# A transformer layer's seam of branch and output products: gates' products ahead of low parts, the last merged tile by halves, VectorE and ScalarE in written order into the first pair

## The chip, the cores and the metric

The kernel runs on one core of a Trainium2 chip, in one launch. The time is device microseconds, the median of several runs. The engines of the core are named as the profile names them: PE (TensorE, matrix products; PEld is its weight load), DVE (VectorE), ACT (ScalarE), POOL (GpSimd) and SP (SyncE, which issues most transfers). Each engine works through its own queue in order and waits by semaphores for the others. Products accumulate in PSUM, tiles live in SBUF, weights and inputs in HBM.

## The reference, cut to what matters

One layer of a diffusion transformer in float32, 1024 tokens by 1024 channels: two attention branches (windowed A, global B), merged by sigmoid gates, an output projection, a layer norm, and a convolutional feed-forward net with a second layer norm. The change lies where the branches are merged and projected:

```python
def _merge_branches(o_a, o_b, gate_logits, w_branch_a, w_branch_b, w_out):
    g_a, g_b = jnp.split(jax.nn.sigmoid(gate_logits), 2, axis=-1)
    return (g_a * (o_a @ w_branch_a) + g_b * (o_b @ w_branch_b)) @ w_out
...
        y = _latent_token_mixer(h, kv_ctx, w_in[l], ...)
        x = _layer_norm(DEEPNORM_ALPHA * x + gate1 * y, ln1_g[l], ln1_b[l])
```

## The kernel before, in words

**Layout.** Channels lie on the 128 partitions, so the 1024 channels are eight tiles, numbered f = 0 to 7, each 128 x 1024 (tokens along the row). The two token halves of 512 are hsl(0) and hsl(1); slice(0, T) is the whole row.

**Float32 by three products.** A float32 operand is split into a high part (a cast to a shorter format, `fp32r`) and a low part (the operand less its high part). `split` (L368 the cast, L373 the low part) does this for weights. `mm3` multiplies high by high (L376), high weight by low operand (L377) and low weight by high operand (L378).

**Branch products and merge.** `bT[0, f]` holds gate A times branch A's product already. `bT[1, f]` is loaded with gate B's sigmoid (the tiles sgd). For f = 0 to 3 only the second token half of branch B's product is left when the seam begins: `group` makes it in PSUM, `gmul` (L1117) multiplies it into `bT[1, f]` on DVE. For f = 4 to 7 `both` makes both halves (tile b, 24 matmuls of 512 columns), and L1418 multiplies it by the gate. Then `merge` adds the two branches on DVE (L1369) and casts the sum to its high part mh on ACT (L1371), and `msplit` makes the low part ml on DVE (L1376). "Gate f" below means this product of tile f.

**The output product.** y = merged times w_out: `y_pair(f, s)` makes two of the eight output tiles for the token range s, in one PSUM tile, with mh and ml of all eight merged tiles as operands. The first pair goes for both of its outputs through merged tiles 0 to 5 first and then through 6 and 7. The weight of output f is loaded as rwo, cast to hwo on ACT (L368), its low part lwo made on DVE (L373), all by `wout_start(f)`, which also loads two tiles of x, z (L1364), and scales them on POOL (L1365): L1532 adds y to them later, and the first layer norm follows.

**Slots.** `ht` hands out the oldest free one of some 35 SBUF slots, `hput` returns one. A load into a slot waits for the last reader of what lay there.

**What sets the order.** Inside a `manual_schedule` block the engines named keep the order in which the code is written; elsewhere a scheduler orders each queue. Before, one block, branch, holds all five engines from the split of w_b's weights up to the last msplit; PE alone is held again from just ahead of the output products.

**nmod and grd.** L1956 makes a small tile nmod (used by the second layer norm at the end of the kernel), and L1983 stores half of it transposed, in pieces of four bytes, to the DRAM tile grd.

Of the kernel before, what the change touches and what calls it, by code (L numbers as in the profile page):

```python
# [7 lines left out]
F32 = mybir.dt.float32  # L8
R32 = mybir.dt.float32r
AF = mybir.ActivationFunctionType  # L10
ALU = mybir.AluOpType
# [4 lines left out]
T = 1024  # L16
NC = 256
KT = 8
# [335 lines left out]
def layer_kernel(  # L354
# [6 lines left out]
    nc = tc.nc  # L361
# [59 lines left out]
    def ht(name, shape=(P, T), dt=F32):  # L421
        hslot[name] = pool, tag = hfree.pop(0)
        return pool.tile(list(shape), dt, tag=tag, name=name, bufs=1)

    def hput(*names):
        for n in names:
            hfree.append(hslot.pop(n))
# [51 lines left out]
    def hsl(hf):  # L479
        return slice(hf * HALF, (hf + 1) * HALF)  # L480
# [39 lines left out]
    for n in (0, 1):  # L520
        s = slice(n * HALF, (n + 1) * HALF)
# [11 lines left out]
    for k in range(KT):  # L533
# [5 lines left out]
        for t in range(NT):  # L539
            s = slice(t * P, (t + 1) * P)  # L540
# [436 lines left out]
    order = []  # L977
# [22 lines left out]
    for n, (gi, k, a) in enumerate(steps):  # L1000
# [21 lines left out]
        for t in tiles:  # L1022
            if t < NT:
                s = slice(t * P, (t + 1) * P)
                x = hT[k][0][:, s], hT[k][1][:, s]
            else:
                s = slice((t - NT) * P, (t - NT + 1) * P)
# [67 lines left out]
    bT, wab, bacc = {}, {}, {}  # L1095
# [252 lines left out]
    mrg = []  # L1348
    zt_ = {}

    def zv(f, s):
        hf = s.start // HALF
        return zt_[f % 4, hf][:, f // 4, s.start - hf * HALF:s.stop - hf * HALF]
# [3 lines left out]
    def wout_start(f, rtag="raw"):  # L1357
        wts[f] = weight(w_out[f], f"wo{f}", 8, tag=None if f < 4 else "wd" if f & 2 else "w", he=nc.scalar,
                        le=nc.vector, rtag=rtag)
        for hf in (0, 1):  # L1360
            if f < 4:
                zt_[f, hf] = ht(f"z{f}_{hf}", (P, 2, HALF))
            z = zv(f, hsl(hf))
            nc.sync.dma_start(z, xT[f][:, hsl(hf)])  # L1364
            nc.gpsimd.tensor_scalar(out=z, in0=z, scalar1=ALPHA, scalar2=0.0, op0=ALU.mult, op1=ALU.add)  # L1365

    def merge(f):
        m = bT[0, f]
        nc.vector.tensor_tensor(out=m, in0=m, in1=bT[1, f], op=ALU.add)  # L1369
        mh, ml = ht(f"mh{f}", dt=R32), ht(f"ml{f}", dt=R32)  # L1370
        nc.scalar.copy(mh, m)  # L1371
        mrg.append((mh, ml))

    def msplit(f):
        mh, ml = mrg[f]
        nc.vector.tensor_tensor(out=ml, in0=bT[0, f], in1=mh.bitcast(F32), op=ALU.subtract)  # L1376
        hput(f"bT0_{f}", f"bT1_{f}")

    wb = {2: [wq.tile([P, 8, P], R32, tag="w", name=f"{a}wb2", bufs=4) for a in "hl"]}
    branch = ExitStack()  # L1380
    branch.enter_context(tc.manual_schedule(engines={mybir.EngineType.PE, mybir.EngineType.DVE, mybir.EngineType.SP,
                                                     mybir.EngineType.Activation, mybir.EngineType.Pool}))
    split(rwb[2], *wb[2], nc.scalar, nc.gpsimd)
    hput("rwb2")

    def both(f):
        ps = big(f"b1_{f}")
        w = wb[f // 2]
        for hf in (0, 1):
            for j in range(4):  # L1390
                k = (f % 2) * 4 + j
                a = O[1, hf, 0, j // 2][:, j % 2], O[1, hf, 1, j // 2][:, j % 2]
                mm3(ps[:, hsl(hf)], (w[0][:, k], w[1][:, k]), a, j == 0, j == 3)
        return ps
# [7 lines left out]
    for f in range(KT):  # L1402
        if f < 4:
            group(1, f, 1, sml(f"b1_{f}_1"))
            gmul(1, f, 1)
            if f:
                msplit(f - 1)
            if f == 1:
                wb[3] = weight(w_b[3], "wb3", 8, he=nc.scalar, le=nc.gpsimd, rtag=None)
            if f == 3:  # L1410
                later(6)
                later(7)
        else:
            ps = both(f)
            msplit(f - 1)
            if f in (5, 7):
                wout_start(f // 2 - 2, None)
            nc.vector.tensor_tensor(out=bT[1, f], in0=ps, in1=bT[1, f], op=ALU.mult)  # L1418
        merge(f)
    msplit(KT - 1)  # L1420
    branch.close()
    opool.release()

    post = tc.alloc_tile_pool(name="post", bufs=1, side="left", reuse_waits="tile")
# [207 lines left out]
    def y_pair(f, s, first=False):  # L1632
        w = s.stop - s.start
        ps = big(f"y{f}_{s.start}_{w}")
        for ks in (range(6), range(6, KT)) if first and s.start == 0 else (range(KT),):
            for a in (0, 1):
                mm_ticked(ps[:, a * HALF:a * HALF + w], wts[f + a], mrg, s, ks)
        for a in (0, 1):
            wout_z(f + a, s, ps[:, a * HALF:a * HALF + w], first and a == 0)

    def ln1(si):
        return ln_steps(zs, zq, LN1_S[si], f"a{si}", emit1, LN1_F[si], *LN1_D[si], order=(0, 4, 1, 5, 2, 6, 3, 7))

    order = ctx.enter_context(ExitStack())
    order.enter_context(tc.manual_schedule(engines={mybir.EngineType.PE}))
    for f in range(0, KT, 2):
        if f + 2 < KT:
            for a in (2, 3):
                wout_start(f + a)
        y_pair(f, hsl(0), f == 0)  # L1650
    pend += ln1(0)
    for f in (0, 2):
        y_pair(f, hsl(1), f == 0)
# [131 lines left out]
    for k in range(4):  # L1785
        steps = build(k)
        n = 2 if k < 2 else 0
# [244 lines left out]
    s = LN2_S[-1]  # L2032
# [181 lines left out]
```

## Time and profile before

| what | value |
|---|---|
| median of 3 runs | 1527.97 us (1526.24 to 1531.01) |
| the profiled execution | 1527.93 us, span 1526.1 us |
| mean granted TensorE clock | 0.998 |
| PE busy | 1510.1 us, 99% |
| DVE busy | 1146.5 us, 75% |
| ACT, POOL busy | 799.2 us, 779.4 us |
| last products of branch B (tile b) | from 735.7 us to 768.3 us after the start |
| first output pair (tile y) | from 768.3 us to 782.8 us |

All times on the timeline are microseconds from the span's start. In a row of the timeline stand start, duration, engine, line, operation, output and inputs (without buffer numbers), shape, and in brackets the idle time before it and what ended it. In the list of waits stand who waited for whom, the total, how often, and the longest.

### The profile page before, as it was taken

The page shows a single profiled execution, that of the slowest core. Times are in us where ns is not written, and L with a number is a line of the kernel's source. Part 1 is how long each engine was busy: PE and PEld are TensorE (multiplying, and loading weights), DVE is VectorE, ACT ScalarE, POOL GpSimd, SP SyncE. Part 2 cuts the span into 40 slices and gives each one's busy share as a digit, 9 for nine tenths or more (in the row PEclk, how much of TensorE's full clock was granted, in tenths as well). Part 3 has the DMA queues.
Part 4 walks back from the last instruction along what each step waited for, and adds up shares of the span by engine and source line. Part 5 has one row for each costly group of instructions (what it writes and reads, how often), then busy time and mean ns, then how long its engine had stood idle before and what let it go on. Part 6 is the DMA issues. An engine that isn't in the chain of part 4 may idle for free.

```text
span 1526.1 us, 21981 instructions
## 1 busy us (share of the span) xinstructions
PE 1510.1 (99%) x7652; PEld 1269.0 (83%) x7652; DVE 1146.5 (75%) x1727; ACT 799.2 (52%) x1403; POOL 779.4 (51%) x743
## 2 busy tenths in 40 slices
PE   9999999999999999999999999999999999999997
PEld 7888888889988888888878998888888888888786
DVE  7588847629777777787656888888888887657797
ACT  5422223449987777788233574444444444435533
POOL 0365303428896566585513556666676664021063
PEclk9999999999999999999999999999999999999999
DMA  9667663312447654723460323333344446996723
GB/s 378 242 230 255 213 233 118 100 38 68 116 112 179 169 126 103 179 59 113 145 154 30 108 83 110 111 111 110 111 110 111 109 111 191 370 270 205 249 83 111
DMA packets 112161, 229.73 MB, mean 151 GB/s; under 512 B 13521, under 2 KB 27345, under 8 KB 111954
## 3 DMA queue, kind: packets, MB, share of 16 engines
q1 hardware_dynamic: 97040, 199.72, 39.8%
q0 software_dynamic: 10400, 20.19, 8.6%
q10 hardware_dynamic: 4610, 8.42, 1.5%
q8 instruction: 60, 0.98, 0.3%
q14 instruction: 51, 0.42, 0.1%
HBM read 177.09 MB, written 65.87 MB: 159 GB/s over the span
## 4 chain that ended last, share of the span: by engine, by line
PE 90%; DVE 4%; DMA 2%; POOL 1%; issue 1%; ACT 1%; SPq 0%; DVEq 0%; POOLq 0%; ACTq 0%
PE av L851 7%; PE pt L842 6%; PE g L378 4%; PE g L377 4%; PE g L376 4%; PE p L377 3%; PE p L378 3%; PE p L376 3%; PE s L754 3%; PE s L755 3%; PE c L377 2%; PE d L377 2%; PE a L377 2%; PE c L376 2%; PE d L376 2%; PE a L376 2%
## 5 line engine op out<-in xcount | busy, mean ns | idle before, releaser
L1226 DVE TENSOR_TENSOR lo<-pt,hi 128x512 fp32r<-128x512 f32 x188 | 126.8, 687 | 44.1 <-ACT hi L1220 33.8
L373 DVE TENSOR_TENSOR ld<-rd,hd 128x1024 fp32r<-128x1024 f32 x77 | 97.5, 1284 | 50.2 <-ACT hd L368 48.1
L1220 ACT CAST hi<-pt 128x512 fp32r<-128x512 f32 x188 | 108.3, 581 | 42.0 <-PE pt L842 23.1
L368 ACT CAST hd<-rd 128x1024 fp32r<-128x1024 f32 x77 | 79.5, 1050 | 86.1 <-PE p L378 59.1
L851 PE MATMUL av<-hi,VT 128*128 128x512 f32 x236 | 104.2, 443 | 0.2 <-POOL hi L1215 0.2
L377 PE MATMUL p<-ld,hd 128*128 128x512 f32 x264 | 102.8, 390 | 0.9 <-DVE ld L373 0.9
L376 PE MATMUL p<-hd 128*128 128x512 f32 x264 | 103.4, 392 | 0.0
L378 PE MATMUL p<-hd,ld 128*128 128x512 f32 x264 | 102.7, 389 | 0.0
L378 PE MATMUL g<-hh,wlg 128*128 128x512 f32 x256 | 99.7, 390 | 0.4 <-POOL wlg L373 0.4
L376 PE MATMUL g<-hh,whg 128*128 128x512 f32 x256 | 100.0, 390 | 0.0
L377 PE MATMUL g<-hl,whg 128*128 128x512 f32 x256 | 99.6, 389 | 0.0
L851 PE MATMUL av<-lo,VT 128*128 128x512 f32 x236 | 99.3, 422 | 0.1
L373 POOL TENSOR_TENSOR wlg<-wg,whg 128x512 fp32r<-128x512 f32 x32 | 45.1, 1413 | 103.4 <-ACT whg L368 98.7
L788 DVE TENSOR_SCALAR_CACHE_REDUCE p<-s,cvt,nmc 128x1024 f32<-128x1024 f32 x64 | 85.6, 1339 | 11.0 <-PE s L755 7.0
L842 PEld LDWEIGHTS pt<-ident,p 128*128 128x128 f32 x512 | 63.5, 140 | 17.6 <-ACT rb L824 0.4
L797 ACT ACTIVATE p<-p,nm 128x1024 f32<-128x1024 f32 x64 | 73.9, 1155 | 7.0 <-DVE p L788 6.5
L842 PE MATMUL pt<-ident,p 128*128 128x128 f32 x512 | 76.6, 272 | 0.1
L368 ACT CAST wS<-s 128x512 fp32r<-128x512 f32 x76 | 45.3, 620 | 53.3 <-POOL s L1546 52.5
L754 PE MATMUL s<-KL,q 128*128 128x512 f32 (+2 forms) x186 | 72.9, 392 | 0.0
L788 DVE TENSOR_SCALAR_CACHE_REDUCE pa<-s,negsink 128x640 f32<-128x640 f32 (+1 forms) x58 | 49.3, 853 | 29.2 <-PE s L755 28.7
L755 PE MATMUL s<-KL,q 128*128 128x512 f32 (+2 forms) x186 | 69.5, 374 | 0.0
L368 ACT CAST wA<-ru 128x512 fp32r<-128x512 f32 x57 | 35.5, 623 | 59.6 <-PE d L378 31.2
(436 smaller groups left out, 5034.4 us busy)
## 6 DMA issues: line engine op xcount, KB each, us to landing
wml<-in_wmodT_dram SPq DMA_DIRECT2D x48, 512.0 KB
ru<-in_w_up_dram SPq DMA_DIRECT2D x38, 512.0 KB
rd<-td SPq DMA_DIRECT2D x55, 256.0 KB
rd<-sd SPq DMA_DIRECT2D x44, 256.0 KB
rd<-in_w_dn_dram SPq DMA_DIRECT2D x33, 256.0 KB
wm<-in_wmodT_dram SPq DMA_DIRECT2D x16, 512.0 KB
wg<-in_w_g_dram SPq DMA_DIRECT2D x32, 256.0 KB
q<-q SPq DMA_DIRECT2D x64, 128.0 KB
```

What stands on the lines that cost most here:

```text
L368: cast[:] = [nc.scalar.copy(hi, src).ins]
L373: low[:] = [lo_eng.tensor_tensor(out=lo, in0=src, in1=hi.bitcast(F32), op=ALU.subtract).ins]
L376: nc.tensor.matmul(ps, a[0], b[0], start=start, stop=False, skip_group_check=resumed)
L377: nc.tensor.matmul(ps, a[0], b[1], start=False, stop=False, skip_group_check=resumed)
L378: return nc.tensor.matmul(ps, a[1], b[0], start=False, stop=stop, skip_group_check=resumed).ins
L754: nc.tensor.matmul(o, self.q1[:, hs], ks, start=True, stop=False)
L755: nc.tensor.matmul(o, self.q2[:, hs], ks, start=False, stop=stop)
L788: nc.vector.tensor_scalar(out=p if self.br else p[:, self.pad + 1:SINK + 1], in0=self.sv[h], scalar1=self.scale()[:, hs] if self.br else - ...
L842: nc.tensor.transpose(tr[:, h * P:(h + 1) * P], src, ident)
L851: nc.tensor.matmul(self.av, v, self.parts[n][low], start=first, stop=self.left == 0)
L1220: nc.scalar.copy(hi, units[u].parts[n])
L1226: e.tensor_tensor(out=lo, in0=src, in1=hi.bitcast(F32), op=ALU.subtract)
```

## The change

Four things are rewritten, and no product is added or removed.

- For f = 4 to 7 the product is multiplied by the gate ahead of the previous tile's low part, no longer behind it.
- The last tile (f = 7) goes through multiplication, merge, cast and low part in two halves of 512 tokens.
- The first two output weights are started in other places: w_out 0 behind merge 4, w_out 1 ahead of gate 6's product, each before in the middle of tiles 5 and 7.
- The written order now holds DVE and ACT into the first pair of y, SP and POOL as before up to the last msplit, and PE without a gap. So five small operations on modc and lnx, which the scheduler used to put far earlier, now stand behind the last ml.

```diff
-    def merge(f):
+    def merge(f, s):
         m = bT[0, f]
-        nc.vector.tensor_tensor(out=m, in0=m, in1=bT[1, f], op=ALU.add)
-        mh, ml = ht(f"mh{f}", dt=R32), ht(f"ml{f}", dt=R32)
-        nc.scalar.copy(mh, m)
-        mrg.append((mh, ml))
-
-    def msplit(f):
+        if s.start == 0:
+            mrg.append((ht(f"mh{f}", dt=R32), ht(f"ml{f}", dt=R32)))
+        nc.vector.tensor_tensor(out=m[:, s], in0=m[:, s], in1=bT[1, f][:, s], op=ALU.add)
+        nc.scalar.copy(mrg[f][0][:, s], m[:, s])
+
+    def msplit(f, s=slice(0, T)):
         mh, ml = mrg[f]
-        nc.vector.tensor_tensor(out=ml, in0=bT[0, f], in1=mh.bitcast(F32), op=ALU.subtract)
-        hput(f"bT0_{f}", f"bT1_{f}")
+        nc.vector.tensor_tensor(out=ml[:, s], in0=bT[0, f][:, s], in1=mh[:, s].bitcast(F32), op=ALU.subtract)
+        if s.stop == T:
+            hput(f"bT0_{f}", f"bT1_{f}")
 
-    branch = ExitStack()
-    branch.enter_context(tc.manual_schedule(engines={mybir.EngineType.PE, mybir.EngineType.DVE, mybir.EngineType.SP,
-                                                     mybir.EngineType.Activation, mybir.EngineType.Pool}))
+    order = ctx.enter_context(ExitStack())
+    order.enter_context(tc.manual_schedule(engines={mybir.EngineType.PE}))
+    branch, inner = ExitStack(), ExitStack()
+    branch.enter_context(tc.manual_schedule(engines={mybir.EngineType.DVE, mybir.EngineType.Activation}))
+    inner.enter_context(tc.manual_schedule(engines={mybir.EngineType.SP, mybir.EngineType.Pool}))
...
         else:
+            if f == 6:
+                wout_start(1, None)
             ps = both(f)
-            msplit(f - 1)
-            if f in (5, 7):
-                wout_start(f // 2 - 2, None)
-            nc.vector.tensor_tensor(out=bT[1, f], in0=ps, in1=bT[1, f], op=ALU.mult)
-        merge(f)
-    msplit(KT - 1)
-    branch.close()
+            for s in [hsl(0), hsl(1)] if f == KT - 1 else [slice(0, T)]:
+                nc.vector.tensor_tensor(out=bT[1, f][:, s], in0=ps[:, s], in1=bT[1, f][:, s], op=ALU.mult)
+                if s.start == 0:
+                    msplit(f - 1)
+                merge(f, s)
+            if f == 4:
+                wout_start(0, None)
+            continue
+        merge(f, slice(0, T))
+    for n in (0, 1):
+        msplit(KT - 1, hsl(n))
+    inner.close()
...
-    order = ctx.enter_context(ExitStack())
-    order.enter_context(tc.manual_schedule(engines={mybir.EngineType.PE}))
     for f in range(0, KT, 2):
         if f + 2 < KT:
             for a in (2, 3):
                 wout_start(f + a)
         y_pair(f, hsl(0), f == 0)
+        if f == 0:
+            branch.close()
```

PE's own order stays the same, row for row. The other queues move as follows; in the names, the last number is a buffer number.

DVE at the end of the branch, before: the last two gates (bT1_7 out of b1_7 is the multiplication, bT0_7 the merge), the low parts ml, and the low parts of output weights lwo.

```order
L1376 TENSOR_TENSOR ml6_8830<-bT0_6_5361,mh6_8829 128x1024
L373 TENSOR_TENSOR lwo1_8861<-rwo1_8858,hwo1_8860 128x1024
L1418 TENSOR_TENSOR bT1_7_8721<-b1_7_8832,bT1_7_8721 128x1024
L1956 TENSOR_SCALAR nmod_13047<-modc_60 128x8
L1369 TENSOR_TENSOR bT0_7_5724<-bT0_7_5724,bT1_7_8721 128x1024
L373 TENSOR_TENSOR lwo2_8893<-rwo2_8890,hwo2_8892 128x1024
L1376 TENSOR_TENSOR ml7_8873<-bT0_7_5724,mh7_8872 128x1024
L373 TENSOR_TENSOR lwo3_8905<-rwo3_8902,hwo3_8904 128x1024
```

DVE at the same place now, from the multiplication of gate 7's first half on (lwo1 stands four rows ahead of it).

```order
L1421 TENSOR_TENSOR bT1_7_8725<-b1_7_8848,bT1_7_8725 128x512
L1966 TENSOR_SCALAR nmod_13054<-modc_60 128x8
L1376 TENSOR_TENSOR ml6_8845<-bT0_6_5361,mh6_8844 128x1024
L1371 TENSOR_TENSOR bT0_7_5724<-bT0_7_5724,bT1_7_8725 128x512
L1421 TENSOR_TENSOR bT1_7_8725<-b1_7_8848,bT1_7_8725 128x512
L1371 TENSOR_TENSOR bT0_7_5724<-bT0_7_5724,bT1_7_8725 128x512
L1376 TENSOR_TENSOR ml7_8876<-bT0_7_5724,mh7_8875 128x512 x2
L1436 TENSOR_SCALAR modc_60<-modc_60 128x8
L1437 TENSOR_TENSOR lnx_68<-ln1c_66,modc_60 128x8
L1438 TENSOR_TENSOR lnx_68<-ln1c_66,modc_60 128x8
L1439 TENSOR_TENSOR lnx_68<-lnx_68,modc_60 128x8
L1440 TENSOR_SCALAR lnx_68<-ln1c_66 128x16
```

lwo2 follows behind these rows: ml7 now stands ahead of it, in halves, and the five small operations between.

ACT at the same place, before: casts of merged tiles (mh) and of output weights (hwo).

```order
L1371 CAST mh5_8798<-bT0_5_5058 128x1024
L1371 CAST mh6_8829<-bT0_6_5361 128x1024
L368 CAST hwo1_8860<-rwo1_8858 128x1024
L368 CAST hwo2_8892<-rwo2_8890 128x1024
L1371 CAST mh7_8872<-bT0_7_5724 128x1024
```

ACT now.

```order
L1372 CAST mh5_8801<-bT0_5_5058 128x1024
L368 CAST hwo1_8807<-rwo1_8805 128x1024
L1372 CAST mh6_8844<-bT0_6_5361 128x1024
L1372 CAST mh7_8875<-bT0_7_5724 128x512 x2
L368 CAST hwo2_8898<-rwo2_8896 128x1024
```

hwo1 moved ahead of mh6, and hwo2 behind mh7.

SP before, from the load of z for outputs 3 and 7 on (rwo are output weights, z tiles of x, grd the store of nmod).

```order
L1364 DMA z3_1_8911<-in_xT_dram 128x512 x2
L1333 DMA rwo2_8890<-in_w_out_dram 128x1024
L1333 DMA rwo3_8902<-in_w_out_dram 128x1024
L1364 DMA z3_0_8908<-in_xT_dram 128x512
L1333 DMA rwo4_8970<-in_w_out_dram 128x1024
L1364 DMA z3_0_8908<-in_xT_dram 128x512
L1333 DMA rwo5_8980<-in_w_out_dram 128x1024
L1333 DMA rwo6_9049<-in_w_out_dram 128x1024
L1983 DMA grd_13052<-nmod_13047 128x4x1
L1333 DMA rwo7_9059<-in_w_out_dram 128x1024
```

SP now.

```order
L1364 DMA z3_0_8914<-in_xT_dram 128x512 x2
L1333 DMA rwo2_8896<-in_w_out_dram 128x1024
L1333 DMA rwo3_8908<-in_w_out_dram 128x1024
L1364 DMA z3_1_8917<-in_xT_dram 128x512
L1333 DMA rwo4_8977<-in_w_out_dram 128x1024
L1364 DMA z3_1_8917<-in_xT_dram 128x512
L1993 DMA grd_13059<-nmod_13054 128x4x1
L1333 DMA rwo5_8987<-in_w_out_dram 128x1024
L1333 DMA rwo6_9056<-in_w_out_dram 128x1024
L1333 DMA rwo7_9066<-in_w_out_dram 128x1024
```

The store grd moved ahead of rwo5 and rwo6. The slot of the z3 tile that comes first is now that of gate 5's bT tile (free after merge 5), before that of gate 6's (free after merge 6). Ahead of these rows, rwo1 moved in front of two of the loads of z; its slot is free after POOL's low part of w_b's weight 2, before after merge 0.

## The prediction

> **What bounds the kernel now.** I read the page first: its span, and how much of it each engine was busy.
>
> ```profile
> span 1526.1 us, 21981 instructions
> PE 1510.1 (99%) x7652; PEld 1269.0 (83%) x7652; DVE 1146.5 (75%) x1727; ACT 799.2 (52%) x1403; POOL 779.4 (51%) x743
> ```
>
> TensorE (PE) is busy for 99% of the span. The change removes no matmul, so it can gain only what PE waits for. The second view is the list of PE's own waits over the whole span (total, times, longest, in us):
>
> ```profile
> PE y L377 <- DVE ml L1376: 1.4, 1, 1.4
> ...
> PE y L376 <- ACT mh L1371: 1.0, 1, 1.0
> PE p L377 <- DVE ld L373: 0.9, 1, 0.9
> ...
> PE y L378 <- DVE lwo L373: 0.3, 1, 0.3
> ```
>
> Three of these waits belong to tile y, the first output product, which is the seam that the change names. The third view is the timeline of PE there: start, duration, and in brackets the idle time before.
>
> ```profile
> 768.32 0.39 PE L376 MATMUL y<-mh,hwo 128*128 128x512 f32 x1
> ...
> 772.63 0.39 PE L377 MATMUL y<-ml,hwo 128*128 128x512 f32 x1
> 773.35 0.50 PE L378 MATMUL y<-mh,lwo 128*128 128x512 f32 x1 [0.33 <-DVE lwo L373]
> ...
> 777.56 0.39 PE L378 MATMUL y<-mh,lwo 128*128 128x512 f32 x1
> 779.00 0.50 PE L376 MATMUL y<-mh,hwo 128*128 128x512 f32 x1 [1.05 <-ACT mh L1371]
> 780.86 0.50 PE L377 MATMUL y<-ml,hwo 128*128 128x512 f32 x1 [1.36 <-DVE ml L1376]
> ...
> 782.78 0.39 PE L376 MATMUL y<-mh,hwo 128*128 128x512 f32 x1
> ```
>
> From 768.32 to 772.63 stand 19 matmuls, 0.2268 us each. The first pair is 48 matmuls, so without waits it would take 10.89 us and end at 779.21. The next pair starts at 782.78. The seam costs **3.57 us**, more than the 2.74 us of bracketed idle time, because pipelined matmuls overlap. It has three parts: the jump to 773.35 costs 0.49, the one to 779.00 costs 1.21, the one to 780.86 costs 1.63; the rest is the slow restarts. PE waits for lwo1, then for mh7, then for ml7.
>
> Why are these late? VectorE (DVE) first, then ScalarE (ACT):
>
> ```profile
> 738.60 0.69 DVE L1117 TENSOR_TENSOR bT<-b,bT 128x512 f32<-128x512 f32 x1 [2.03 <-PE b L378]
> ...
> 752.83 1.21 DVE L1369 TENSOR_TENSOR bT<-bT,bT 128x1024 f32<-128x1024 f32 x1
> 755.15 1.23 DVE L1376 TENSOR_TENSOR ml<-bT,mh 128x1024 fp32r<-128x1024 f32 x1 [1.11 <-ACT mh L1371]
> 756.30 1.22 DVE L1418 TENSOR_TENSOR bT<-b,bT 128x1024 f32<-128x1024 f32 x1
> 757.55 1.22 DVE L1369 TENSOR_TENSOR bT<-bT,bT 128x1024 f32<-128x1024 f32 x1
> 759.89 1.22 DVE L1376 TENSOR_TENSOR ml<-bT,mh 128x1024 fp32r<-128x1024 f32 x1 [1.12 <-ACT mh L1371]
> 761.03 1.22 DVE L373 TENSOR_TENSOR lwo<-rwo,hwo 128x1024 fp32r<-128x1024 f32 x1
> 762.17 1.22 DVE L1418 TENSOR_TENSOR bT<-b,bT 128x1024 f32<-128x1024 f32 x1
> ...
> 773.21 1.22 DVE L1418 TENSOR_TENSOR bT<-b,bT 128x1024 f32<-128x1024 f32 x1
> 774.34 0.17 DVE L1956 TENSOR_SCALAR nmod<-modc 128x8 f32<-128x8 f32 x1
> 774.46 1.64 DVE L1369 TENSOR_TENSOR bT<-bT,bT 128x1024 f32<-128x1024 f32 x1
> 778.03 1.23 DVE L373 TENSOR_TENSOR lwo<-rwo,hwo 128x1024 fp32r<-128x1024 f32 x1 [1.93 <-ACT hwo L368]
> 779.18 1.63 DVE L1376 TENSOR_TENSOR ml<-bT,mh 128x1024 fp32r<-128x1024 f32 x1
> ```
>
> ```profile
> 758.81 1.05 ACT L1371 CAST mh<-bT 128x1024 fp32r<-128x1024 f32 x1 [3.68 <-DVE bT L1369]
> 759.76 1.04 ACT L368 CAST hwo<-rwo 128x1024 fp32r<-128x1024 f32 x1
> ...
> 776.95 1.05 ACT L368 CAST hwo<-rwo 128x1024 fp32r<-128x1024 f32 x1 [5.10 <-DMA rwo<-in_w_out_dram]
> 777.90 1.04 ACT L1371 CAST mh<-bT 128x1024 fp32r<-128x1024 f32 x1
> ```
>
> Two things are to be seen. Before every ml, DVE stands idle for about 1.1 us until ACT has cast mh, while the next product already waits: the product for gate 7 was complete when PE turned to y at 768.32, and DVE multiplied it at 773.21. And at the end the order is unlucky: merge 7 is finished at 776.10, but ACT stands at the head of hwo2 until that weight's transfer lands (776.95), so mh7 starts at 777.90; DVE then does lwo2 ahead of ml7.
>
> **The change part by part.** *Products ahead of low parts* (tiles 4 to 7). No instruction is added; the multiplication fills the gap before ml. Up to merge 3 (752.83) the order is the old one. Product 4 is ready (72 matmuls before 768.32, about 752.2), so it is multiplied at 753.98 (one back-to-back step is 1.14 to 1.15, as from 761.03 to 762.17), ml3 stays at 755.15, merge 4 comes at 756.30, 1.25 earlier.
>
> *lwo0 and lwo1 directly behind merges 4 and 5.* This adds a wait: DVE now stands from the merge through mh and hwo. By the rows the steps are 1.26 (757.55 to 758.81), 0.95 (to 759.76) and 1.08 (776.95 to 778.03), so 3.29 from merge to lwo. Behind the waiting lwo are the multiplication, ml and merge of the next tile. The times that follow: lwo0 759.59, multiplication 5 760.73, ml4 761.87, merge 5 763.01; lwo1 766.30, multiplication 6 767.44, ml5 768.58, merge 6 769.72.
>
> *The last tile in halves.* One 128x1024 multiplication, merge and ml become two each, one cast becomes two. A half multiplication costs 0.69 (row 738.60). A half cast from SBUF has no row for mh; the nearest, same form and line L368, is on the page:
>
> ```profile
> L368 ACT CAST wS<-s 128x512 fp32r<-128x512 f32 x76 | 45.3, 620 | 53.3 <-POOL s L1546 52.5
> ```
>
> So halving costs some 0.2 us of DVE in all. Multiplication 7 of half 0 at 770.86; mh6 ends at 772.03 (1.26 and 1.05 behind merge 6), ml6 772.06; merge 7 of half 0 773.20, then half 1's two steps at 0.7 each; mh7 of half 0 ends at 774.6; its ml7 runs 775.3 to 776.0, half 1's ends by 776.8. PE, unstalled, wants lwo1 at 772.85 (20 matmuls into the pair), mh7 at 777.16 (39) and ml7 at 777.39 (40), all of half 0 only. Margins: lwo1 5.4, mh7 2.6, **ml7 1.4 us**. All three waits go.
>
> *What is late next.* hwo2 and lwo2 stand behind the halves, and so do the five small operations on modc and lnx, which used to run far earlier. Five steps of 0.12 (774.34 to 774.46) are 0.6 us at least, and two of them read what the one before wrote, so I take 1.0. lwo2 ends at about 779.0, and PE wants it at 768.32 + 50 x 0.2268 = 779.66. **Margin 0.7 us**, the smallest. Its transfer is no limit any more: in the queue of SyncE (SP) rwo2 now stands behind z3_0, which waits for merge 5 (about 764.2), not for merge 6.
>
> *GpSimd's scaling of z* is reordered, and rwo1 is loaded ahead of two z loads. Here the trace shows a price:
>
> ```profile
> 744.62 0.68 DVE L1117 TENSOR_TENSOR bT<-b,bT 128x512 f32<-128x512 f32 x1
> 745.89 2.74 DVE L1376 TENSOR_TENSOR ml<-bT,mh 128x1024 fp32r<-128x1024 f32 x1 [0.59 <-ACT mh L1371]
> 745.15 2.41 POOL L373 TENSOR_TENSOR lwb<-rwb,hwb 128x1024 fp32r<-128x1024 f32 x1
> 774.41 0.62 POOL L1365 TENSOR_SCALAR z<-z 128x512 f32<-128x512 f32 x1 [0.64 <-DMA z<-in_xT_dram]
> ```
>
> An ml beside GpSimd's lwb took 2.74 instead of 1.22; merge 7 beside the z scaling of 774.41 took 1.64, 0.42 more; the multiplication out of PSUM took its plain 0.68. Between merge 4 and lwo2 the new order has eight z scalings. If none hits DVE the cost is 0; less than 0 is excluded, since PE has no other wait here to win. If four do, 1.7 us, less the 0.7 margin, is 1.0 on PE. A burst of the worst kind moved onto the path (1.52 for the ml and three times 0.42, 2.8 us) would leave 2.1. I take 0.2, near the low end, since DVE has two waits of about 2.1 us (757.44 to 759.59 and again for hwo1) in which a scaling hits nothing.
>
> The Trainium skill's page "SBUF — State Buffer", section "Who interferes with whom", has it harder: a VectorE instruction with two SBUF inputs and a GpSimd one that reads SBUF exclude each other, and the later one blocks fully. The 2.74 agrees (lwb ends at 747.56, and 1.07 us later so does the ml); the 0.42 of merge 7 is less than the whole scaling. By that rule it is the extreme case, rival (d) below, that has to be feared, and the sum would be 1528.6.
>
> *Slots.* Which shared slot a tile gets (ht) changes with the order of the calls, and so do the waits of rwo1 and of the z loads. I price that at nothing: rwo1 is issued behind GpSimd's lwb2 instead of merge 0, some 5 us earlier, and the z tiles are read only when the first pair's result is taken out, after 779. lwb3 comes later by the load of one weight, and PE wants it only with gate 6, 10.9 us before 768.32; it was done at 747.56. If that cover of 9.9 us were gone, PE would wait at gate 6 one for one.
>
> **Sum.** 3.57 gained less 0.2 is 3.4 us. The profiled execution took 1527.93 (span 1526.1, 1.8 around it), which is the median of the runs (1527.97) but for 0.04. Forecast **1524.5 us**.
>
> **The rivals.** *(a) The scalings give part back*: four hits to a worst burst, 1.0 to 2.1 us of the gain lost, 1525.4 to 1526.5, say 1526.0. For it: 1.64 and 2.74. Against it: DVE's two waits.
>
> *(b) Slower, through grd.* In SP's queue the transfer of nmod in 4-byte pieces (grd) now goes ahead of rwo5, rwo6 and rwo7 instead of rwo7 alone. Rows of SP, of two stretches (last column GB/s) and of the cast that waited for rwo7:
>
> ```profile
> 782.35 0.43 SPq L1983 DMA_DIRECT2D grd<-nmod  x1
> 783.52 0.33 SPq L1333 DMA_DIRECT2D rwo<-in_w_out_dram  x1
> 788.00:790.00 2.00, 2.00 (x10) 1.69 (x9) 0.00 (x0) 0.00 (x0) 0.04 (x1) 1.00 1.37 47
> 796.00:798.00 2.00, 2.00 (x11) 1.65 (x10) 0.00 (x0) 0.63 (x1) 0.00 (x0) 1.00 0.88 340
> 797.37 1.05 ACT L368 CAST hwo<-rwo 128x1024 fp32r<-128x1024 f32 x1 [5.20 <-DMA rwo<-in_w_out_dram]
> ```
>
> Beside grd the transfers fall to 47 GB/s, and rwo7 needed 13.8 us. In the new order grd is issued at about 774.5 (ml6 ends at 773.3, then three loads of 0.33 to 0.43), rwo5 at about 779 (it needs lwo2's buffer). With 13.8 us it lands at 792.8; PE wants hwo5 at 768.32 + 120 x 0.2268 = 795.5, and the cast takes 1.05. So 1.6 us are to spare. It turns slower from a landing after 797.9 on, 18.9 us after issue. If grd holds two such stretches, 27.6 us, PE waits 12.2 us and the time is 1536.7. Against it: by 796 the rate was back at 340 GB/s, 13.6 us after grd was issued, which here is 788.
>
> *(c) Nothing moves*: what PE gains is lost at a later wait, 1527.9. Against it: of PE's waits only the 0.9 for ld and one of 0.3 lie behind the seam, so nothing is in sight that would hold the shift.
>
> *(d) Full blocking*: each of the eight scalings gets in ahead of a DVE instruction and holds it for its whole 0.62. DVE is 5.0 us late, less the margin of 0.7 is 4.3, and the time 1528.6. For it: the 2.74, where ml got going only at about 747.5. Against it: 0.42 at the z scaling, and DVE's waits.
>
> **How the numbers follow.** The likeliest case, waits gone, 0.68: 1524.4 to 1525.3. (a) 0.14, (b) 0.06, (c) 0.09, (d) 0.03. 0.3% is 4.6 us, about what a measurement of this kernel can tell from no change; the three runs before lie 4.8 apart, so a median of after can fall 1 to 2 us off the forecast. Even the whole seam, 3.57, is inside 0.3%: faster by more needs luck of 1.1 us on top, about one in four of the likeliest case and little elsewhere, 0.19; slower by more, (b) and bad draws of (c) and (d), 0.07; within, 0.74. The range 1522.0 to 1528.2 takes in (a), most of (c), and that scatter.
>
> **What would show it.** Right: in the list of PE's waits no y row is left, or a lwo row under 0.5; y's second pair starts 10.9 to 11.1 us after the first; DVE multiplies the product of gate 7 by halves at about 771 and 774; mh7 of half 0 ends before 776; GB/s drops from about 775 on, not from 786. Wrong: a y row for ml7 or lwo2 above 1 us with DVE rows of 1.6 and more in front of it (a); a wait for hwo5 near 795 (b); y without waits and the span the same (c); every DVE row of ml and merge between 757 and 779 at 1.8 (d).

## The result, and the profile after

The changed kernel takes **1523.44 us** (median, 1522.49 to 1525.0); the kernel before, run beside it, 1528.6 us (1524.24 to 1531.01). The ratio is **0.9971, 95% interval 0.9961 to 0.9981**, so it is faster by 0.29%, just inside the 0.3% that the prediction set as the bound of "the same"; the interval takes in that bound. The profiled execution took 1522.49 us, 1520.7 of it span.

First the page of the changed kernel, its first two lines; then the list of TensorE's (PE's) own waits, complete.

```profile
span 1520.7 us, 21983 instructions
PE 1508.5 (99%) x7652; PEld 1268.6 (83%) x7652; DVE 1145.2 (75%) x1730; ACT 799.6 (53%) x1404; POOL 781.4 (51%) x743
```

```profile
PE cb L519 <- DVE mhalf L404: 1.1, 1, 1.1
PE g L378 <- POOL wlg L373: 0.4, 1, 0.4
PE zt L2052 <- DVE zz L1915: 0.3, 1, 0.3
PE av L851 <- POOL hi L1215: 0.2, 1, 0.2
```

No row of y is left, and the 0.9 us for ld, far behind the seam, is gone too. The timeline of PE in the seam shows the first matmul of the first pair, the first of the second, and the only one that was still touched, two matmuls into the second pair, where PE takes lwo2:

```profile
767.98 0.39 PE L376 MATMUL y<-mh,hwo 128*128 128x512 f32 x1
...
778.86 0.39 PE L376 MATMUL y<-mh,hwo 128*128 128x512 f32 x1
...
779.31 0.43 PE L378 MATMUL y<-mh,lwo 128*128 128x512 f32 x1
779.58 0.39 PE L376 MATMUL y<-mh,hwo 128*128 128x512 f32 x1
```

The first pair lasts 10.88 us, as without any wait; before it lasted 14.46. VectorE (DVE) and ScalarE (ACT) in the same stretch:

```profile
766.22 1.30 DVE L373 TENSOR_TENSOR lwo<-rwo,hwo 128x1024 fp32r<-128x1024 f32 x1 [2.06 <-ACT hwo L368]
...
769.71 1.63 DVE L1371 TENSOR_TENSOR bT<-bT,bT 128x1024 f32<-128x1024 f32 x1
771.26 0.68 DVE L1421 TENSOR_TENSOR bT<-b,bT 128x512 f32<-128x512 f32 x1
...
775.53 1.46 DVE L1376 TENSOR_TENSOR ml<-bT,mh 128x512 fp32r<-128x512 f32 x2
...
777.55 2.77 DVE L373 TENSOR_TENSOR lwo<-rwo,hwo 128x1024 fp32r<-128x1024 f32 x2
```

```profile
774.32 0.62 ACT L1372 CAST mh<-bT 128x512 fp32r<-128x512 f32 x1 [1.89 <-DVE bT L1371]
775.65 0.62 ACT L1372 CAST mh<-bT 128x512 fp32r<-128x512 f32 x1 [0.71 <-DVE bT L1371]
776.17 2.00 ACT L368 CAST hwo<-rwo 128x1024 fp32r<-128x1024 f32 x2
...
789.29 1.05 ACT L368 CAST hwo<-rwo 128x1024 fp32r<-128x1024 f32 x1 [8.59 <-DMA rwo<-in_w_out_dram]
```

Product 7 is multiplied at 771.26, not at 773.21; mh7 starts at 774.32, not at 777.90; ml7 follows at 775.53; hwo2 and hwo3 come behind, at 776.17, and no longer wait for a transfer. The row at 777.55 holds lwo2 and lwo3; lwo2 alone took 1.64 instead of 1.22, beside a z scaling on GpSimd (POOL) that began at 777.50.

Where did the 5.4 us between the two spans come from? I cut both traces at the first output product (y), at the first product of the stage after it (u), and at the first and the last down product (p). The rows below are PE's stretches (start and end, length, busy time of PE, PEld, DVE, ACT, POOL, then the granted clock, DMA share and GB/s), of before and of after.

```profile
768.30:864.60 96.30, 93.56 (x509) 80.23 (x507) 64.46 (x82) 37.27 (x52) 36.40 (x26) 1.00 0.34 94
864.60:1296.00 431.40, 431.33 (x1975) 359.90 (x1975) 364.68 (x361) 216.15 (x308) 274.52 (x167) 1.00 0.39 115
1296.00:1479.90 183.90, 182.96 (x811) 150.53 (x810) 131.28 (x129) 89.66 (x96) 36.62 (x27) 1.00 0.79 247
```

```profile
768.00:860.80 92.80, 92.80 (x509) 80.34 (x508) 65.22 (x90) 36.34 (x53) 36.89 (x27) 1.00 0.34 92
860.80:1292.10 431.30, 431.27 (x1974) 359.93 (x1974) 363.16 (x361) 216.14 (x308) 273.35 (x167) 1.00 0.39 115
1292.10:1474.60 182.50, 182.50 (x811) 150.70 (x810) 131.89 (x129) 89.56 (x96) 36.60 (x27) 1.00 0.79 249
```

The seam gave 3.5 us (96.3 to 92.8), as forecast. Another 1.4 (183.9 to 182.5) lies 500 us later among the down products, where nothing was changed, 0.3 lies ahead of y, and 0.1 each in the stage of u and in the tail. And the medians lie 5.2 apart, not 3.4. The experiments had to say which parts of the change were needed, whether the change has anything to do with the 1.4, and why the medians differ by more than the seam.

### The profile page after: what moved, and what is told of

The parts are those of the page before. It is cut to its first block, busy times and chain, and to the rows that moved or that the text cites. A ratio compares the mean times of both kernels' runs of the same rounds, so it can differ in the third digit from the quotient of the medians.

```text
span 1520.7 us, 21983 instructions
## 1 busy us (share of the span) xinstructions
PE 1508.5 (99%) x7652; PEld 1268.6 (83%) x7652; DVE 1145.2 (75%) x1730; ACT 799.6 (53%) x1404; POOL 781.4 (51%) x743
## 4 chain that ended last, share of the span: by engine, by line
PE 91%; DVE 5%; DMA 2%; issue 1%; POOL 1%; ACT 0%; SPq 0%; DVEq 0%; ACTq 0%; POOLq 0%
PE av L851 7%; PE pt L842 7%; PE g L378 4%; PE g L377 4%; PE g L376 4%; PE s L754 3%; PE s L755 3%; PE c L377 2%; PE d L377 2%; PE a L377 2%; PE c L376 2%; PE a L376 2%; PE d L376 2%; PE d L378 2%; PE a L378 2%; PE c L378 2%
```

## The experiments

All the kernels at a glance. "y to u" is the stretch of the first row above; "u to end" is the span less the start of u. The last column counts the executions whose mean granted TensorE clock was 0.997 or less. The medians come from four comparisons, in which the kernel before took 1528.6, 1527.06, 1527.83 and 1527.93 us; so medians of different comparisons can lie more than a microsecond apart without a cause in the kernels.

| kernel | median us | y to u | u to end | PE's waits in y | at 0.997 or less |
|---|---|---|---|---|---|
| before (first profile) | 1528.6 | 96.3 | 661.5 | 1.4, 1.0, 0.3 | 45 of 86, in the three later comparisons |
| before, again | 1528.1 | 96.9 | 660.0 | 1.4, 0.6 | 8 of 12 |
| new | 1523.44 | 92.8 | 659.9 | none | 2 of 10 |
| new, again | 1522.76 | 92.9 | 661.1 | none | 0 of 9 |
| low parts first | 1525.93 | 95.3 | 660.2 | 0.8, 0.5, 0.4 | 3 of 12 |
| last tile whole | 1523.87 | 93.1 | 663.0 | none | 5 of 12 |
| lwo0, lwo1 at the old place | 1522.55 | 92.7 | 659.4 | none | 2 of 12 |
| the same, again | 1522.78 | 92.7 | 660.2 | none | 3 of 10 |
| seam order alone, on before | 1523.97 | 92.9 | 662.4 | none | 2 of 7 |
| seam order undone | 1522.35 | 93.2 | 658.8 | none | 0 of 5 |
| grd twice | 1523.93 | 92.8 | 660.6 | none | 0 of 6 |
| grd last | 1523.68 | 92.7 | 662.3 | none | 4 of 8 |
| z scaled twice | 1524.95 | 96.8 | 660.0 | 1.6 | 1 of 8 |
| ml7 six times | 1527.95 | 96.9 | 659.4 | 2.3 | 10 of 12 |

**The kernel before, again** (no edit).

> The kernel before, unchanged, profiled a second time. Two things are asked of its trace. First, the seam: theory T1 (the gain is the 3.57 us of the seam) says the first pair again lasts 14.1 to 14.8 us where it would take 10.89 unstalled. Second, the stage of the down products, where PE waited 0.9 us for ld in the first profile of before and not at all in the profile of after: if that wait is scatter of when the loads land, it comes out at another size here, between 0 and 2 us, and the time from the first down product to the last differs from the first profile's by more than 0.5 us. If instead the change caused its absence (rival T2), it stands here again at 0.7 to 1.1 us. Ratio to the kernel before: 0.999 to 1.001.

Ratio 1.001 (0.9998 to 1.0021). The wait for ld is not there, and the stretch of the down products took 182.5, as in the new kernel; in u to end the fourteen profiles range from 658.8 to 663.0, and kernels that gain in the seam stand at both ends. A wait for ld of 0.6 to 0.9 us is in five of the fourteen profiles, old and new kernels alike. The new kernel, profiled a second time, has the wait that its first profile lacked:

```profile
PE p L377 <- DVE ld L373: 0.8, 1, 0.8
```

So the 1.4 us is scatter, and T2 falls. The seam itself came out at 14.96 us for the first pair, above what I expected, though its waits were smaller. PE's timeline of this profile shows why:

```profile
778.04 0.39 PE L378 MATMUL y<-mh,lwo 128*128 128x512 f32 x1
779.05 0.49 PE L376 MATMUL y<-mh,hwo 128*128 128x512 f32 x1 [0.62 <-ACT mh L1371]
780.91 0.66 PE L377 MATMUL y<-ml,hwo 128*128 128x512 f32 x1 [1.37 <-DVE ml L1376]
781.37 0.63 PE L378 MATMUL y<-mh,lwo 128*128 128x512 f32 x1
...
783.93 0.63 PE L378 MATMUL y<-mh,lwo 128*128 128x512 f32 x1
784.35 0.47 PE L376 MATMUL y<-mh,hwo 128*128 128x512 f32 x1
784.66 0.39 PE L377 MATMUL y<-ml,hwo 128*128 128x512 f32 x1
```

Behind the wait for ml7 the matmuls start 0.427 us apart instead of 0.227, for 3.4 us, and then go on at the old pace; the granted clock is 0.50 in the two whole microseconds from 782 to 784. From 780.91 to 784.66 stand nine steps, 3.75 us instead of 2.04: the spell costs 1.7. The waits alone cost 2.4 here (0.78 for mh7 and 1.63 for ml7, none for lwo1), against 3.57 in the first profile. So what the first profile had for lwo1 (0.49) was scatter as well, and so was the 0.42 by which a scaling lengthened merge 7: here merge 7 took 1.21.

**Low parts first**: the multiplication goes back behind the low part.

```diff
-                nc.vector.tensor_tensor(out=bT[1, f][:, s], in0=ps[:, s], in1=bT[1, f][:, s], op=ALU.mult)
                 if s.start == 0:
                     msplit(f - 1)
+                nc.vector.tensor_tensor(out=bT[1, f][:, s], in0=ps[:, s], in1=bT[1, f][:, s], op=ALU.mult)
```

> The new kernel with one part undone: in tiles 4 to 7 the low part of the tile before is again ahead of the multiplication; everything else as in the new kernel. T1: DVE stands again some 1.1 us before each ml, so merges come later by one multiplication, half 0 of ml7 ends near 777.9 where PE wants it at 777.04 and lwo2 ends near 781 where PE wants it at 779.3. That makes PE rows y <- ml of 0.6 to 1.0 and y <- lwo of 0.5 to 1.2, and a time 1.3 to 2.2 us above the new kernel: 1524.7 to 1525.6 against about 1528.2 of the kernel before, ratio 0.9977 to 0.9983. Rival R1 (the early loading of rwo2 and the order of the casts alone removed the waits): no y row over 0.3 and a time equal to the new kernel's, 1523.4, ratio 0.997.

Ratio 0.999 (0.998 to 0.9999), 2.5 us above the new kernel's median of the first comparison, and the seam's stretch is 2.5 longer (95.3 against 92.8): somewhat more than I expected, since a wait for mh7 came on top. The list of waits:

```profile
PE y L377 <- DVE ml L1376: 0.8, 1, 0.8
...
PE y L376 <- ACT mh L1372: 0.5, 1, 0.5
...
PE y L378 <- DVE lwo L373: 0.4, 1, 0.4
```

R1 falls, but only for this neighbourhood: here lwo0 and lwo1 stand early, and DVE waits 2.06 us ahead of each of them, which the earlier products have to pay for.

**Last tile whole**: one multiplication, merge, cast and low part of 1024 columns.

```diff
-            for s in [hsl(0), hsl(1)] if f == KT - 1 else [slice(0, T)]:
+            for s in [slice(0, T)]:
...
-    for n in (0, 1):
-        msplit(KT - 1, hsl(n))
+    msplit(KT - 1)
```

> The new kernel with the last tile whole again: one multiplication, one merge, one cast mh7 and one ml7 of 1024 columns instead of two of 512. T1: multiplication 7 at 771.3, merge 7 at 773.6 to 774.9, mh7 to 776.0, ml7 at 776.0 to 777.2, PE wants it at 777.04, so one y <- ml row of 0.1 to 0.5; lwo2 ends near 779.0 as in the new kernel. Time 1523.4 to 1524.0, not to be told from the new kernel; ratio 0.9967 to 0.9975. Rival R2 (the halves are what saves the ml7 wait of 1.63): a y <- ml row of 1.2 to 1.6 us and 1525.0, ratio 0.998.

Ratio 0.9979 (0.9969 to 0.999). There is no y wait in the list, and the stretch is 93.1, 0.3 above the new kernel: ml7 ends as PE wants it. R2 falls.

**lwo0 and lwo1 at the old place** (behind ml, in tiles 5 and 7), run twice, the second time beside the new kernel.

```diff
-            if f == 6:
-                wout_start(1, None)
...
                 if s.start == 0:
                     msplit(f - 1)
+                    if f in (5, 7):
+                        wout_start(f // 2 - 2, None)
...
-            if f == 4:
-                wout_start(0, None)
```

> The new kernel with one part undone: lwo0 and lwo1 (their casts, their low parts, and the z loads issued with them) stand again with tiles 5 and 7 behind ml, instead of directly behind merges 4 and 5. Slots and the order of SyncE's loads are then those of the kernel before; the order of products, the halves and the casts are those of the new one. T1: DVE no longer stands twice for 2.1 us, half 0 of ml7 ends near 774, lwo2 near 777, no y row in the list of PE's waits, and since the margins were wide enough before, nothing is won by it: 1523.0 to 1523.9, ratio 0.9965 to 0.9975, the same as the new kernel. Rival T2 (what the new kernel won beside the seam, about 1.5 us behind it, comes from the new slots and loads): 1524.7 to 1525.3, ratio 0.998, with the wait p <- ld of 0.7 to 1.1 back.

> The same kernel as u_wout_back, beside the new kernel on one chip: lwo0 and lwo1 stand again behind ml in tiles 5 and 7. Both have no y wait, so the medians should be equal within 0.8 us; u_wout_back was 0.9 under the new kernel, but on another chip. If the early lwo0 and lwo1 cost something that the list of PE's waits does not show, it is 0.8 to 1.2 lower again.

Ratios 0.9972 (0.9961 to 0.9983) and 0.9968 (0.9957 to 0.998); beside the new kernel 1522.78 against 1522.76. Slots and loads are the old ones here, and nothing of the gain is missing, so T2 falls a second time. Nor does the early lwo pair give anything.

**The seam's order alone, on the kernel before**: ACT casts mh7 ahead of hwo2, DVE takes ml7 ahead of lwo2, the small operations between. The blocks are set up as in the change; the lines that end them are these.

```diff
...
     msplit(KT - 1)
-    branch.close()
+    inner.close()
...
         y_pair(f, hsl(0), f == 0)
+        if f == 0:
+            branch.close()
```

> The kernel before with one part of the change alone: in the seam, ACT casts mh7 ahead of hwo2, and DVE takes ml7 and the five small operations ahead of lwo2. The last tile is whole, products stay behind low parts, weights are loaded as before. T1, from the first profile of before: mh7 776.15 to 777.2 and no wait for it; the wait for lwo1 stays (0.49); ml7 ends at 778.45 to 778.85 where PE, that much later, wants it at 777.9, which costs 0.55 to 1.2; lwo2 ends at 780.3, in time. The seam then costs 1.0 to 1.7 instead of 3.57, the stretch from the first y to the first u is 93.8 to 94.5 us (96.3 before, 92.8 in the new kernel), and the time is 1.9 to 2.5 us under the kernel before, ratio 0.9982 to 0.9990. Rival R3 (the wait only goes over to lwo2, which now comes later): a y <- lwo row of 1 us or more, 95.5 us or more from y to u, ratio 0.9994 to 1.0005.

Ratio 0.998 (0.9967 to 0.9993): the better part of the gain with this one edit, and in the profile all of the seam but 0.1. I had left 1.0 to 1.7 of it, 0.49 of that for lwo1, which was in time here as in the second profile of the kernel before. DVE and PE of this profile:

```profile
773.83 1.22 DVE L1369 TENSOR_TENSOR bT<-bT,bT 128x1024 f32<-128x1024 f32 x1
776.16 1.23 DVE L1376 TENSOR_TENSOR ml<-bT,mh 128x1024 fp32r<-128x1024 f32 x1 [1.11 <-ACT mh L1371]
```

```profile
777.20 0.39 PE L376 MATMUL y<-mh,hwo 128*128 128x512 f32 x1
777.45 0.50 PE L377 MATMUL y<-ml,hwo 128*128 128x512 f32 x1
```

Merge 7 took 1.22 where it had taken 1.64 before, since the scaling of z did not fall on it, and ml7 ended at 777.39, just as PE came to it. That is a margin of nothing: with the 0.42 of before PE would have waited. R3 falls: no wait for lwo2. The edit moves mh7, ml7 and the small operations together; which of these moves does it was not tried.

**The seam's order undone**, on the new kernel: hwo2 ahead of mh7, lwo2 ahead of ml7.

```diff
     inner.close()
+    branch.close()
...
-        if f == 0:
-            branch.close()
```

> The new kernel with one part undone: ACT again casts hwo2 ahead of mh7's first half and hwo3 between the halves, and DVE takes lwo2 ahead of ml7. rwo2 is still loaded early. T1 (what mattered was that rwo2's transfer stood in front of mh7): rwo2 has landed by 771 to 772, so hwo2 runs 772.4 to 773.4 while DVE still merges, mh7's half 0 starts at 774.3 as in the new kernel, lwo2 775.5 to 776.7, half 0 of ml7 776.7 to 777.4 where PE wants it at 777.04: a y <- ml row of 0.2 to 0.5, from the first y to the first u 93.0 to 93.5 us, 0.2 to 0.7 above the new kernel, 1523.6 to 1524.2. Rival R4 (the order of the casts itself is what counts): y <- ml of 1.0 or more, 94.2 us or more from y to u, 1524.8 or more.

Ratio 0.9967 (0.9954 to 0.998), the stretch 93.2, 0.4 above the new kernel; the list of waits has no y row, only one slow matmul where ml7 comes in. ACT's hwo2, ahead of mh7, waits for no transfer any more:

```profile
772.48 1.05 ACT L368 CAST hwo<-rwo 128x1024 fp32r<-128x1024 f32 x1
774.47 0.63 ACT L1372 CAST mh<-bT 128x512 fp32r<-128x512 f32 x1 [0.94 <-DVE bT L1371]
```

R4 falls. So there are two cures, and each does nearly all of it without the other: either mh7 no longer stands behind hwo2, which waits for rwo2, and ml7 no longer behind lwo2; or rwo2 is there early, products come earlier and the last tile goes by halves, so that hwo2 doesn't wait. The second cure is the rest of the change together; whether the early rwo2 does it alone was not tried.

**z scaled twice**: sixteen more scalings on GpSimd (POOL).

```diff
             nc.gpsimd.tensor_scalar(out=z, in0=z, scalar1=ALPHA, scalar2=0.0, op0=ALU.mult, op1=ALU.add)
+            nc.gpsimd.tensor_scalar(out=z, in0=z, scalar1=1.0, scalar2=0.0, op0=ALU.mult, op1=ALU.add)
```

> The new kernel with every z scaled a second time on GpSimd (by 1.0, in place), 16 more operations of 0.62 us; between merge 4 and lwo2 about eight more. If a scaling costs a DVE instruction beside it some 0.4 us, as in the profile of before, and only those beside it, then two to five DVE rows between 757 and 779 are at 1.5 to 1.7 instead of 1.22, ml7 or lwo2 comes 0.4 to 1.5 later, PE waits 0 to 1.2 in y, and the stretch from the first y to the first u is 92.8 to 94.0 us. If each scaling holds DVE for its whole length (rival (d)), DVE is some 5 us late, PE waits 3 us or more, and that stretch is 95.8 us or more.

Ratio 0.998 (0.9969 to 0.999), 1.5 above the new kernel's median of the first comparison. A row each of GpSimd, DVE (three) and PE:

```profile
755.95 1.56 POOL L1366 TENSOR_SCALAR z<-z 128x512 f32<-128x512 f32 x1
...
756.95 1.63 DVE L1372 TENSOR_TENSOR bT<-bT,bT 128x1024 f32<-128x1024 f32 x1
...
763.30 1.21 DVE L1377 TENSOR_TENSOR ml<-bT,mh 128x1024 fp32r<-128x1024 f32 x1
764.43 1.63 DVE L1372 TENSOR_TENSOR bT<-bT,bT 128x1024 f32<-128x1024 f32 x1
...
779.67 0.74 PE L377 MATMUL y<-ml,hwo 128*128 128x512 f32 x1 [1.58 <-DVE ml L1377]
```

Both pay: a scaling that meets a DVE instruction takes 1.46 to 1.56 instead of 0.62, and the next DVE instruction out of SBUF 0.36 to 0.41 more. From merge 4 to ml7 that happened to seven DVE rows, 2.8 us in all, and the margin was spent and PE waited 1.6. That is past my 0 to 1.2, because more rows were hit than I thought; the price of one hit was right, and it is not the 0.62 of rival (d). The stretch of 96.8 looks like (d)'s, but has a half-pace spell behind the wait, as above; the median shows only 1.5.

**grd twice** and **grd last**: the store of nmod in 4-byte pieces a second time, into a buffer of its own; and in another kernel once, but behind rwo7 (wdma holds the loads of the weights).

```diff
...
             nc.sync.dma_start(grd.rearrange("f p -> p f"), nmod[:, 0:4])
+            nc.sync.dma_start(grd2.rearrange("f p -> p f"), nmod[:, 0:4])
```

```diff
...
-            nc.sync.dma_start(grd.rearrange("f p -> p f"), nmod[:, 0:4])
+            with tc.issue_after(wdma["wo7"]):
+                nc.sync.dma_start(grd.rearrange("f p -> p f"), nmod[:, 0:4])
```

> The new kernel with one more transfer of nmod in 4-byte pieces, into a buffer of its own, directly behind grd and so ahead of rwo5. It prices rival (b) and the margin that the prediction gave to hwo5. If grd is what takes the queue's rate down for some 13 us each time, the low stretch lasts from 775 to about 801 instead of 788, rwo5 lands at 800 to 803 instead of 789.3, PE, which wants hwo5 at about 795, waits 5 to 9 us for it, the stretch from the first y to the first u is 98 to 102 us instead of 92.8, and the time is 1529 to 1533. If the low rate is from something else at that time, rwo5 lands at 789 to 791, PE waits nowhere, and the time is 1523.4.

> The new kernel with the transfer of nmod in 4-byte pieces (grd) issued behind rwo7 instead of ahead of rwo5; nothing else moves. If grd is what takes the rate down to 30 to 50 GB/s for about ten microseconds, rwo5, issued at 779.2, lands at 782 to 785 instead of 789.3, rwo7 by 789, and the low stretch comes after that, from about 785 on, and delays the first of the next stage's weights. If the low rate comes from something else at 780 to 788, rwo5 lands at 787 to 790 as before. The time is 1523.4 either way, since PE wants hwo5 only at 795.

Ratios 0.9974 (0.9962 to 0.9986) and 0.9975 (0.996 to 0.999), both without a y wait. ACT's cast of hwo5 with grd twice, and then with grd last:

```profile
790.20 1.05 ACT L368 CAST hwo<-rwo 128x1024 fp32r<-128x1024 f32 x1 [10.55 <-DMA rwo<-in_w_out_dram]
```

```profile
782.26 1.05 ACT L368 CAST hwo<-rwo 128x1024 fp32r<-128x1024 f32 x1 [3.19 <-DMA rwo<-in_w_out_dram]
```

Three stretches of two microseconds with grd last (last column GB/s):

```profile
782.00:784.00 2.00, 2.00 (x10) 1.65 (x10) 1.29 (x2) 1.74 (x3) 1.84 (x2) 1.00 0.92 336
...
788.00:790.00 2.00, 2.00 (x11) 1.65 (x10) 0.00 (x0) 0.00 (x0) 0.00 (x0) 1.00 0.76 47
790.00:792.00 2.00, 2.00 (x10) 1.68 (x9) 0.00 (x0) 0.00 (x0) 0.00 (x0) 1.00 0.59 31
```

So grd is the cause of the low rate: sent last, it leaves rwo5 alone (782.26 instead of 789.29), and the low stretch moves behind. But a second one adds 0.9 us (1.3 against PE, whose y began 0.4 earlier), not the 11 to 14 that I had priced. That twice the pieces take twice the time, as I had expected of this run, is wrong.

**ml7 six times**, and **the new kernel again**: in the first, the low part of half 0 of the last tile is computed six times in place, to put a wait back into the seam.

```diff
-        nc.vector.tensor_tensor(out=ml[:, s], in0=bT[0, f][:, s], in1=mh[:, s].bitcast(F32), op=ALU.subtract)
+        for n in range(6 if f == KT - 1 and s.start == 0 else 1):
+            nc.vector.tensor_tensor(out=ml[:, s], in0=bT[0, f][:, s], in1=mh[:, s].bitcast(F32), op=ALU.subtract)
```

> The new kernel with the low part of the last tile's half 0 computed six times in place instead of once, so that PE waits again in the seam: half 0 of ml7 ends near 778.9 where PE wants it at 777.04, a wait of 1.7 to 2.1; lwo4 comes ahead of lwo2 on DVE, lwo2 ends near 783.5 where PE then wants it at 781.3, a wait of 1.8 to 2.5. From the first y to the first u 96.4 to 97.6 us, as much as before the change. T3: 5 or more of 12 runs at a mean clock of 0.997 or less, and a median 4.2 to 6 us above the new kernel, at the kernel before or higher, 1527.5 to 1529.5. T4: the share is that of the new kernel (at most 3 of 12), and the median is 3.6 to 4.8 us above the new kernel's at whatever clock.

> The new kernel, unchanged. From the first y to the first u 92.7 to 92.9 us, no y row in the list of PE's waits. Two theories on why the medians lie 4.4 to 5.2 us apart although the seam costs 3.57. T3 (a PE wait in the seam is now and then followed by a spell in which TensorE runs at half pace, which lowers the mean granted clock of the run; the new kernel has no such wait): at most 4 of 12 runs here have a mean clock of 0.997 or less, against about half of the runs of the kernel before, and at the clock 0.998 the medians lie 3 to 4 us apart. T4 (spells fall anywhere and only the seam counts): the two kernels have the same share of runs at 0.997 or less.

Ratios to the kernel before 1.0002 (0.9991 to 1.0013) and 0.9964 (0.9946 to 0.9981). PE's timeline with the wait put back:

```profile
779.76 0.79 PE L377 MATMUL y<-ml,hwo 128*128 128x512 f32 x1 [2.29 <-DVE ml L1377]
780.35 0.63 PE L378 MATMUL y<-mh,lwo 128*128 128x512 f32 x1
...
782.48 0.63 PE L377 MATMUL y<-ml,hwo 128*128 128x512 f32 x1
```

A spell at half pace stands behind the wait again, and the wait for lwo2 that I had expected did not arise, since PE came to it later. Of the executions 10 of 12 had a mean clock of 0.997 or less, of the new kernel none of 9, of the kernel before 18 of 30, all on one chip. The medians: 1527.95, 1522.76, 1527.93. At a mean clock of 0.998 they are 1526.01, 1522.76 and 1525.47. So the equal share that T4 expected is not there, and T3 holds in its direction: of the 5.2 between the two, 3.3 stands at equal clock (from two executions only), and the rest goes with the clock. My "3 to 4 us apart at 0.998" came out at 2.7 for the kernel before, which fits the 2.4 of waits in its second profile. Against all the kernels without a y wait that ran beside it, taken together, it was 2.6 (1525.49 against 1522.87), 3.1 (1526.22 against 1523.16) and 3.0 (1525.47 against 1522.52) in the three later comparisons.

Of the fourteen profiles four have a y wait above 1 us, and three of these a spell behind it; the other ten have no spell in the seam. But T4 is right in one point, that spells fall elsewhere too. In three profiles (last tile whole, seam order alone, grd last) one stands between 1457.9 and 1462.7, among the down products, again with a granted clock of 0.50 and some 3.4 us long. In these three, and in no other, PE waited 0.25 to 0.29 us for zq, among matmuls of one column, 1.9 to 2.8 us ahead of the spell:

```profile
1457.49 0.38 PE L1503 MATMUL stb<-onec,zq 128*128 128x1 f32 x2 [0.29 <-DVE zq L1470]
```

These are also the three with the longest "u to end" (662.3 to 663.0), and kernels without a y wait can have executions at 0.997 or less by such spells.

## Why the prediction was right

It said 1524.5, range 1522.0 to 1528.2, and "within 0.3%" as the likeliest; measured were 1523.44 and 0.29%. That the ratio fell on this side of 0.3% is luck, with an interval from 0.19% to 0.39%.

- *The seam costs 3.57 and all three waits go.* Right for the two profiles set side by side: 3.5 from y to u, no y row left. The 3.57 is one profile's figure; the second had 2.4 of waits and a spell of 1.7.
- *The times on DVE and ACT.* PE's first y came 0.34 earlier than in the profile before; less that, lwo0, multiplication 5, merge 5, lwo1 and merge 6 came within 0.35 us of the steps. From there 0.7 later: merge 6 at 769.71 took 1.63, one hit by a scaling.
- *GpSimd's scaling of z*, charged 0.2. It cost DVE some 0.4 twice, at merge 6 and at lwo2 itself (1.63 and 1.64 instead of 1.22), of seven scalings that ran between merge 4 and lwo2. That used up the margin of 0.7 at lwo2, the smallest: lwo2 ended at 779.19, and PE lost about 0.05, at 779.31. The run with doubled scalings shows that the term was rightly taken as a risk, and that its price is per hit.
- *Full blocking (d)*. The Trainium skill's page "SBUF — State Buffer", section "Who interferes with whom", says that the later of the two instructions blocks fully. The rows agree more than I thought: GpSimd's 1.46 to 1.56 for 0.62 is a wait for DVE's instruction to end, and DVE's 0.36 to 0.41 most of a scaling. What was wrong in (d) was its count, eight in a row; two rows were hit.
- *Slots*, priced at nothing. Right: with the old slots the time is the same.
- *Rival (b)*. grd as the cause of the low rate is shown. The two stretches, 27.6 us, that its 1536.7 rests on were not seen: rwo5 was cast 10.1 us after its issue (779.22 to 789.29), before PE wanted hwo5 at 795. The rate fell from 778 on (66 GB/s from 778 to 780), 3 us after grd was issued, not from 775.
- *The parts of the change.* The prediction didn't ask which part is needed. The seam's order suffices by itself, and so does the rest of the change without it; the halves gain 0.3 us of the stretch, and the early lwo0 and lwo1 gain nothing and need the earlier products.

**The step that was mis-sized** is the sum: "3.57 gained less 0.2 is 3.4 us", set against the profiled execution as if that stood for the median. The medians lie 4.5 to 5.2 apart (1528.6 to 1523.44; on the last chip 1527.93 to 1522.76; the first kernel with lwo0 and lwo1 at the old place, 1527.06 to 1522.55, 4.5). The missing term is what follows a wait: in some executions a spell at half pace, 1.7 us each. The profile of before had none behind its waits; it had the 1.4 of the late ld instead, and so met the median to 0.04 by other terms than an execution in the middle has. I took that for a confirmation. In the time itself two misses partly cancelled: against the ten runs of before (1528.6) the start was 0.7 too low, and the gain 1.8 too small.

What stays open is what decides whether a wait is followed by a spell: 1.36 us was not (first profile of before), 1.37, 1.58 and 2.29 were; and the kernel with z scaled twice, with a wait of 1.6, had only 1 of 8 executions at 0.997 or less. Waits of 0.9 for ld had none behind them, and the three of 0.25 to 0.29 for zq had one each. Open too are the parts inside each of the two cures.

## What to carry to other kernels

Ask of a wait on the bound engine which single instruction in the queue ahead is itself waiting, here one cast for a late weight. Taking mh7 and ml7 out from behind this cast and the low part that follows it won nearly the whole seam; so did the rest of the rewrite without that, in which the transfer and the products come earlier. Look at more than one profile of the same kernel before reading a wait of one microsecond as the kernel's, and don't take it for proof that a profiled execution meets the median. Waits of TensorE can cost more than their length, so judge a cure by medians and clock as well as by the sum of waits.

## What the runs showed of the hardware

- *Half-pace spells.* Matmuls 0.427 instead of 0.227 us apart, at a granted clock of 0.50, for about 3.4 us (780.91 to 784.35 in the kernel before), behind waits of 1.4 to 2.3 us, and 1.9 to 2.8 us behind waits of 0.25 to 0.29 among matmuls of one column. The Trainium skill's page "TensorE: Matmul & The Clock Gate", section "HAM oscillation — how this bites in real kernels", has gaps above some 3.4 us as the ones to avoid. Its section "What's actually happening" states a gate with two rates, full and half, and a window of 3413 ns; the length and the halved rate of the spells agree. Gaps well under 3.4 us were followed by one here.
- *A store in 4-byte pieces holds up more than what is queued behind it.* In the kernel with the seam's order undone, rwo5 was issued ahead of grd, and was late all the same (10.6 us from issue to the cast of hwo5). With grd last the same befell rwo7: issued ahead of grd's 781.72, it was cast only at 792.12. In the kernel with the order undone, SyncE's queue and ACT's cast were:

```profile
776.92 0.33 SPq L1333 DMA_DIRECT2D rwo<-in_w_out_dram  x1
777.29 0.43 SPq L1992 DMA_DIRECT2D grd<-nmod  x1
```

```profile
787.53 1.05 ACT L368 CAST hwo<-rwo 128x1024 fp32r<-128x1024 f32 x1 [7.65 <-DMA rwo<-in_w_out_dram]
```

- *Two such stores, one behind the other, take hardly longer than one*: hwo5 was cast at 790.20 instead of 789.29.
